# First layer: the S5 columns of the input projection multiplied last, the S5 tables behind all column products, the S5 recurrence and its gated output beside the attention

## Chip, cores and metric

The kernel runs on one core of a Trainium2 chip. The time is device microseconds (us) of one execution, the median of several runs. The engines are named as in the profile: PE (TensorE matmul), PEld (its weight load), DVE (VectorE), ACT (ScalarE), POOL (GpSimd) and SP (SyncE, which issues nearly all transfers). Each engine takes its instructions in a fixed order.

## What is computed

Two layers of a decoder trunk over 1024 tokens of width 1024. One input projection feeds four mixers; the third, S5, is a complex diagonal recurrence with a gated output:

```python
h = rms_norm(x, mix_norm[l])
c_q, c_kv, k_pe, lru_x, lru_gate, s5_u, nsa_q, nsa_kv, nsa_gate = jnp.split(h @ w_in[l], IN_SPLITS, axis=-1)
y_a = mla(c_q, c_kv, k_pe, ...)          # multi-head latent attention
y_b = rglru(lru_x, lru_gate, ...)        # gated linear recurrence
y_c = s5(s5_u, ...)                      # 16 groups of 64 complex states
y_d = nsa(nsa_q, nsa_kv, nsa_gate, ...)  # three-branch sparse attention
y = rms_norm(jnp.stack([y_a, y_b, y_c, y_d], axis=2), out_norm[l])
x = x + y.reshape(x.shape) @ w_out[l]
x = x + hier_moe(rms_norm(x, ffn_norm[l]), ...)

def s5(u, ...):
    # tables from the parameters: powers of the discretised a, bb = g * b
    bu = einsum(u, bb); h = scan(h = ab * h + bu)       # complex
    y = gelu(einsum(h, c) + d * u)
    return y * sigmoid(y @ w_glu + b_glu)
```

## The kernel before

`layer(l, src)` (line 1952) writes one layer as Python generators whose `yield`s interleave the work. Where the text says that something is written earlier or later, this is the order of the program's text; the order that each engine runs is fixed when the program is built, and an instruction written later can stand earlier on its engine when it is ready. A tile comes from a group of buffers of fixed number: 16 of kind `p2` (128x512 fp32, line 128), 4 of kind `p4` (128x1024), 8 each of `wh` and `wl`, and in the stages up to the end of the second token products four PSUM banks `ps1` (line 154). A tile takes a buffer before its first write and gives it back after its last read.

The stages of a layer, in the order of the text before the change:

- In the first layer only, `s5_gen(0, True)` (line 665) first issues the loads of the S5 parameters. Its second part, the S5 tables, follows behind the norm: a chain on DVE (powers of the transition, the rotation tables `phases` for two halves, one on DVE and one on POOL, then for each of four blocks the powers `AC` and `G`), PE transposes and small products, and stores to DRAM (`WA`, `TT`, `KP`). Its tiles are nearly all `p2`. For the second layer the same tables are made beside the experts of the first.
- `mixer_norm` (line 436): eight tiles of x are loaded, normalised, transposed and split into a high and a low part (`hT`). Every fp32 product is made of three matmuls of such parts (lines 181 to 183).
- Column products, `mixer_in` (line 463): 7 groups of 128 columns, each in 2 halves of 512 tokens: 14 units of 24 matmuls into one `ps1` bank each. The groups are 864 and 992 (S5), 352 and 480 (input of the linear recurrence, LRU), 608 and 736 (its gate), 1376 (compressed keys and values). S5 columns are copied to `s5u` (`p4`) and go to DRAM `ud`; LRU columns are copied to `lrux` and `lrug`, which are `p2`, and `lru_piece` (line 615) works on them with about ten more `p2` tiles per piece, in four pieces.
- `s5_run` (line 934): four blocks of `s5_block` (line 879), in three steps each: load the tables and multiply U by `WB` into the one `pto` bank, copy and swap halves by DMA; rotate (two POOL multiplies, one DVE add), four scans on DVE, swap, rotate back; two products per group into `pto`, a gelu, and after two blocks a store to DRAM `vd`. One step is taken per `tick` of the column units from the fourth unit on, and the last ones in the token products.
- First token products, `tok_units(l, 0)` and `mixer_in_tok` (lines 479, 499): 8 tiles of 24 matmuls of 364 columns, each copied to a `p2` tile `z`; `prep_mla` works on `z`. `constants2` and `rope_tables` (lines 238, 316) are written before all columns in the first layer, behind the S5 tables.
- Second token products: 8 tiles of 24 matmuls of 512 columns. `s5_out` (line 943), the gated output of S5, is written from the fourth tile of the first token products on, in two halves of 512 tokens: 24 matmuls of 512 columns, tanh, 16 transposes, stores to DRAM `yd`.
- Attention: `mla_stream` and `nsa_stream`, interleaved by `weave` (line 2064), one step of each per turn. Both gather their values in the one bank `pto`; `mla_values` and `nsa_values` (lines 1363, 1243) hold it with the flag `o_busy`. When the MLA stream ends, `mix_stream` (line 1415) takes its turns: `mix_a(i)` reads 128 rows of `yd` (line 1467), norm, output projection, residual, router.
- `router` and `moe`.

Of the kernel before, what the change touches and what calls it, by code (L numbers as in the profile page):

```python
# [102 lines left out]
class Trunk:  # L103
# [359 lines left out]
    def mixer_in(self, l):  # L463

        w = self.I["w_in"][l].rearrange("(k p) n -> p k n", p=128)
        cols = (864, 992, 352, 608, 480, 736, 1376)
        first = [self.wunit(w[:, :, c:c + 128], 8, 128) for c in cols[:4]]
        yield
        hTh, hTl = self.hT
        for col in cols:  # L470
            wh, wl = first.pop(0) if first else self.wunit(w[:, :, col:col + 128], 8, 128)
            for half in range(2):
                acc = self.ps1()
                for k in range(8):
                    self.mm3(acc, wh[:, k, :], wl[:, k, :], hTh[half][k // 4][:, k % 4], hTl[half][k // 4][:, k % 4],
                             k == 0, k == 7)
                yield col, half, acc
# [401 lines left out]
    def s5_block(self, l, b, io):  # L879
# [12 lines left out]
        WB, AC, TR, TI = WA[:, 0], WA[:, 1], TT[:, 0], TT[:, 1]  # L892
        pt = self.pt("o")
# [27 lines left out]
        yield  # L921
        py = self.pt("o")
# [11 lines left out]
    def s5_run(self, l):  # L934

        io = {}
        blocks = [self.s5_block(l, b, io) for b in range(4)]
        for b in (0, 0, 1, 1, 0, 2, 2, 1, 3, 3, 2, None, 3):
            if b is not None:
                next(blocks[b])  # L940
            yield

    def s5_out(self, l, V):
        nc, v = self.nc, self.nc.vector
        r, w = self.raw(), self.raw(dt=F32R)
        nc.sync.dma_start(r[:, 0:512].rearrange("p (k n) -> p k n", k=2),
                          self.I["s5_w_glu"][l].rearrange("(k p) n -> p k n", p=128))
        self.hi(w[:, 0:512], r[:, 0:512])
        self.lo(w[:, 512:1024], r[:, 0:512], w[:, 0:512])
        wh, wl = [w[:, o:o + 512].rearrange("p (k n) -> p k n", k=2) for o in (0, 512)]  # L950
        for hf in range(2):
            Y, Yh, Yl = self.raw(), self.raw(dt=F32R), self.raw(dt=F32R)
            for k in range(2):
                nc.sync.dma_start(Y[:, 512 * k:512 * k + 512].rearrange("p (t n) -> p t n", t=4),
                                  self.vd[128 * k:128 * k + 128, 4 * hf:4 * hf + 4, :])
            self.hi(Yh, Y)
            self.lo(Yl, Y, Yh)
            Y, Yh, Yl = [[t[:, 512 * k:512 * k + 512] for k in range(2)] for t in (Y, Yh, Yl)]
            yield
            for m in range(2):  # L960
                while self.o_busy:
                    yield
                pt = self.pt("o")
                ms = slice(128 * m, 128 * m + 128)
                for k in range(2):
                    self.mm3(pt, wh[:, k, ms], wl[:, k, ms], Yh[k], Yl[k], k == 0, k == 1)
                t = self.p2(name="glut")
                nc.scalar.activation(t, pt, AF.Tanh, bias=V["hglu"][:, m:m + 1], scale=0.5)
                v.scalar_tensor_tensor(Y[m], t, 1.0, Y[m], op0=ALU.add, op1=ALU.mult)
                yield  # L970
            while self.o_busy:
                yield
            for m in range(2):
                pt = self.pt("o")
                for j in range(4):
                    self.T(pt[:, 128 * j:128 * j + 128], Y[m][:, 128 * j:128 * j + 128])
                o = self.p2((128, 4, 128), name="gluo")
                nc.scalar.activation(o, pt.rearrange("p (j c) -> p j c", j=4), AF.Copy, scale=0.5)
                nc.sync.dma_start(self.yd.rearrange("(n t) c -> n t c", t=8)[:, 4 * hf:4 * hf + 4,
                                                                             512 + 128 * m:640 + 128 * m], o)  # L980
            yield

# [478 lines left out]
    def mix_a(self, i):  # L1461

        nc, mp = self.nc, self.mp
        while self.ndone <= i:
            yield
# [486 lines left out]
    def layer(self, l, src):  # L1952
        nc, tc = self.nc, self.tc
        self.hp = Region(self.bg, f"hT{l}", [("r", [(f"hT{a}{k}{j}", 2048, 1)]) for k in range(2) for a in "hl" for j in range(2)])
        xs, s5 = {}, self.s5_run(l)
# [12 lines left out]
        if l == 0:  # L1968
            gen = self.s5_gen(0, True)
            next(gen)  # L1970
# [4 lines left out]
        if l == 0:  # L1975
            next(units)
            for _ in gen:
                pass
            self.constants2()
            self.rope_tables()  # L1980
        V = self.layer_vectors(l)
        for col, half, pt in units:
# [20 lines left out]
            tick(s5 if col != 864 and (col, half) != (992, 0) else iter(()))  # L2003
        us = self.tok_units(l, 0, V)
        self.nsa_compress(l, V)
        for e in self.mixer_in_tok(us):
            if e:
                later(self.prep_mla(l, *e, V), 1, 2, 3, 4)
                if e[0] == 3:
                    us = self.tok_units(l, 1, V)  # L2010
                    s5 = self.chain(s5, self.s5_out(l, V))
                tick(s5)
# [28 lines left out]
        for _ in s5:  # L2041
            pass
# [11 lines left out]
        self.weave(self.chain(mla, self.mix_stream(l, src)), nsa)  # L2054
# [5 lines left out]
    def chain(self, *gens):  # L2060
        for g in gens:
            yield from g

# [69 lines left out]
```

## Time and profile before

| | us |
|---|---|
| median of 3 runs (lowest, highest) | 2161.67 (2157.28, 2170.07) |
| the profiled execution | 2166.39 |
| its span, first to last instruction | 2164.6 |
| PE busy | 1847.8 (85%) |
| DVE busy | 1309.7 (61%) |
| ACT busy | 1131.7 (52%) |
| POOL busy | 667.5 (31%) |

The profile is of one execution, the slowest core (there is one). Busy times overlap; a matmul's end is modelled, so a busy PE is not a PE at its peak. The first layer runs from 0 to some 1100 us, the second from there on; the two run the same stages but for the S5 tables.

### The profile page before, as it was taken

Reading aid. Unit: us, or ns where it says so; the run is one execution under the profiler, and the core shown is the slowest. Engines: PE = TensorE matmul, PEld = TensorE weight load, DVE = VectorE, ACT = ScalarE, POOL = GpSimd, SP = SyncE. Lnnn points to the kernel's source line nnn. Section 1 sums busy time; section 2 is a strip of 40 time slices with the busy share of each in tenths; the row PEclk is TensorE's granted clock in tenths of the full one; section 3 lists DMA queues with packets and bytes.
Section 4 is the critical chain, followed back from the end, with each engine's and each line's share of the span. In section 5 each row is a group of like instructions: output and inputs, shape, how many; then the busy total and the mean of one; then the engine's idle time right before and its main releaser. Section 6 shows DMA issues by size and latency. Waiting matters only on the chain. (4 is left out here: it accounts for less than half of the span.)

```text
span 2164.6 us, 31426 instructions
## 1 busy us (share of the span) xinstructions
PE 1847.8 (85%) x10386; PEld 1508.6 (70%) x10386; DVE 1309.7 (61%) x2895; ACT 1131.7 (52%) x2474; POOL 667.5 (31%) x1130
## 2 busy tenths in 40 slices
PE   4758899999899977888957789989998999679997
PEld 3647876767677766777856678766676677578886
DVE  5976556577755464776734465565776553746664
ACT  4146544566644435565634555455666543347664
POOL 2432463111111126558711224631111111332221
PEclk9979998699899978999987899986999999789999
DMA  7345442113222337898864354311123123489985
GB/s 218 116 104 134 124 123 62 37 53 73 90 76 80 130 130 193 239 252 244 264 155 148 93 128 124 115 59 37 55 72 94 71 81 139 135 231 289 271 258 124
DMA packets 265966, 293.28 MB, mean 135 GB/s; under 512 B 95416, under 2 KB 222264, under 8 KB 265784
## 3 DMA queue, kind: packets, MB, share of 16 engines
q1 hardware_dynamic: 248568, 243.60, 36.5%
q0 software_dynamic: 16640, 46.43, 10.1%
q8 instruction: 87, 1.43, 0.3%
q10 hardware_dynamic: 576, 1.05, 0.1%
q14 instruction: 95, 0.78, 0.1%
HBM read 215.88 MB, written 79.35 MB: 136 GB/s over the span
## 5 line engine op out<-in xcount | busy, mean ns | idle before, releaser
L177 DVE TENSOR_TENSOR wl<-raw,wh 128x512 fp32r<-128x512 f32 (+3 forms) x294 | 214.6, 758 | 112.0 <-ACT wh L169 110.5
L169 ACT ACTIVATE wh<-raw 128x512 fp32r<-128x512 f32 (+3 forms) x294 | 181.7, 657 | 104.6 <-PE ps L182 55.7
L181 PE MATMUL ps<-mo,wh 128*128 128x256 f32 x576 | 171.3, 297 | 25.2 <-ACT mo L169 25.2
L182 PE MATMUL ps<-mo,wh 128*128 128x256 f32 x576 | 167.8, 292 | 0.2 <-DVE mo L177 0.2
L183 PE MATMUL ps<-mo,wl 128*128 128x256 f32 x576 | 166.3, 290 | 0.0
L1199 DVE TENSOR_REDUCE mx<-ps 128x1 f32<-128x640 f32 (+11 forms) x160 | 132.7, 830 | 50.9 <-PE ps L1233 28.3
L181 PEld LDWEIGHTS ps<-mo,wh 128*128 128x128 f32 x576 | 115.4, 200 | 29.2 <-ACT mo L169 29.0
L169 ACT ACTIVATE mo<-ptt 128x512 fp32r<-128x512 f32 x132 | 76.4, 595 | 105.5 <-PE ptt L214 105.5
L177 DVE TENSOR_TENSOR mo<-ptt,mo 128x512 fp32r<-128x512 f32 x132 | 90.4, 686 | 62.1 <-ACT mo L169 61.7
L177 DVE TENSOR_TENSOR ntl<-ptt,at 128x512 fp32r<-128x512 f32 x132 | 89.1, 686 | 55.5 <-ACT at L169 54.8
L1201 ACT ACTIVATE P<-ps,mx 128x640 f32<-128x640 f32 (+7 forms) x128 | 89.2, 698 | 61.6 <-DVE mx L1199 53.9
L169 ACT ACTIVATE at<-ptt 128x512 fp32r<-128x512 f32 x132 | 76.5, 596 | 82.5 <-PE ptt L214 78.2
L182 PEld LDWEIGHTS ps<-mo,wh 128*128 128x128 f32 x576 | 114.8, 199 | 1.3 <-DVE mo L177 0.5
L183 PEld LDWEIGHTS ps<-mo,wl 128*128 128x128 f32 x576 | 114.7, 199 | 0.0
L202 POOL TENSOR_TENSOR rr<-rv,mhalf 128x1 f32<-128x1 f32 (+5 forms) x98 | 102.1, 1042 | 7.8
L181 PE MATMUL ptx<-wh,mo 128*128 128x512 f32 x240 | 100.8, 420 | 3.4 <-ACT ch L1145 1.7
L214 PE MATMUL ptt<-ident,xg 128*128 128x128 f32 x400 | 64.3, 297 | 41.5 <-DMA xg<-hbuf,mo 38.7
L1815 POOL DMA_INDIRECT xg<-hbuf,mo x50 | 58.0, 1159 | 131.5 <-PE ptt L214 67.1
L181 PE MATMUL ps<-wh,hT 128*128 128x364 f32 (+1 forms) x256 | 97.8, 383 | 0.0
L181 PE MATMUL ps<-hT,wh 128*128 128x512 f32 x224 | 93.8, 420 | 3.5 <-ACT wh L169 3.3
L183 PE MATMUL ptx<-wh,mo 128*128 128x512 f32 x240 | 96.2, 401 | 0.0
L182 PE MATMUL ps<-wl,hT 128*128 128x364 f32 (+1 forms) x256 | 96.0, 375 | 0.0
(636 smaller groups left out, 5805.3 us busy)
## 6 DMA issues: line engine op xcount, KB each, us to landing
raw<-in_moe_w_gate_dram SPq DMA_DIRECT2D x96, 256.0 KB
raw<-in_moe_w_up_dram SPq DMA_DIRECT2D x96, 256.0 KB
mo<-in_moe_w_down_dram SPq DMA_DIRECT2D x32, 512.0 KB
raw<-in_moe_w_down_dram SPq DMA_DIRECT2D x32, 512.0 KB
zm<-mqk SPq DMA_DIRECT2D x16, 512.0 KB
at<-zm SPq DMA_DIRECT2D x16, 512.0 KB
wo<-in_w_out_dram SPq DMA_DIRECT2D x16, 512.0 KB
mo<-yd SPq DMA_DIRECT2D x16, 512.0 KB
```

What stands on the lines that cost most here:

```text
L169: self.nc.scalar.activation(out, in_, AF.Copy)
L177: e.tensor_tensor(out, in_, hi.bitcast(F32), op=ALU.subtract)
L181: mm(out, lh, rh, start=start, stop=False)
L182: mm(out, lh, rl, start=False, stop=False)
L183: mm(out, ll, rh, start=False, stop=stop)
L202: g.tensor_tensor(r, v, self.mhalf[:P, 0:1].to_broadcast([P, k]), op=ALU.pow)
L214: self.nc.tensor.transpose(out, in_, self.ident[:k, :k])
L1199: v.tensor_reduce(mx, S3, axis=AX.X, op=ALU.min)
L1201: nc.scalar.activation(P[j][:, 0:n], S3[:, j], AF.Exp, bias=mx[:, j:j + 1], scale=-1.0, accum_out=acc[:, j:j + 1])
L1815: self.nc.gpsimd.indirect_dma_start(out=xg, out_offset=None, in_=self.hbuf[l], in_offset=bass.IndirectOffsetOnAxis(ap=ix, axis=0), bounds_ ...
```

## The change

In the first layer the column groups are multiplied in the order 352, 608, 480, 736, 1376, 864, 992. The loads of the S5 parameters are written behind the norm and the first weight loads. `constants2`, `rope_tables` and the S5 tables are written behind the last column product and before the first token products. No step of S5 is taken before the second token products; there and in the four turns after them it is one per tile, then one per two turns of `weave` (`sparse`). The four blocks run one after the other instead of interleaved.

In both layers `s5_out` works on four quarters of 256 tokens instead of two halves (48 matmuls of 256 columns in place of 24 of 512), with `p2` tiles instead of `raw`; products into `pto` are put off while `o_busy`; the loop that ran S5 out before the attention's second part is gone, and `mix_a` waits until `s5_out` has ended (`s5_done`).

```diff
@@ mixer_in
-        cols = (864, 992, 352, 608, 480, 736, 1376)
+        cols = (864, 992, 352, 608, 480, 736, 1376) if l else (352, 608, 480, 736, 1376, 864, 992)
@@ s5_block (before the product by WB, and again before the last products)
+        while self.o_busy:
+            yield
         pt = self.pt("o")
@@ s5_run
         io = {}
+        if l == 0:
+            for b in range(4):
+                yield from self.s5_block(l, b, io)
+            return
@@ s5_out
-        for hf in range(2):
-            Y, Yh, Yl = self.raw(), self.raw(dt=F32R), self.raw(dt=F32R)
...
+        r, wh, wl = [self.p2((128, 2, 256), dt, name="gl" + n) for n, dt in (("w", F32), ("wh", F32R), ("wl", F32R))]
...
+        for q in range(4):
+            Y = self.p2((128, 2, 256), name="glY")
             for k in range(2):
-                nc.sync.dma_start(Y[:, 512 * k:512 * k + 512].rearrange("p (t n) -> p t n", t=4),
-                                  self.vd[128 * k:128 * k + 128, 4 * hf:4 * hf + 4, :])
+                nc.sync.dma_start(Y[:, k].rearrange("p (t n) -> p t n", t=2),
+                                  self.vd[128 * k:128 * k + 128, 2 * q:2 * q + 2, :])
+            yield
+            Yh, Yl = [self.p2((128, 2, 256), F32R, name="glY" + n) for n in "hl"]
             self.hi(Yh, Y)
             self.lo(Yl, Y, Yh)
             yield
+            while self.o_busy:
+                yield
+            pt = self.pt("o")
             for m in range(2):
                 ms = slice(128 * m, 128 * m + 128)
                 for k in range(2):
-                    self.mm3(pt, wh[:, k, ms], wl[:, k, ms], Yh[k], Yl[k], k == 0, k == 1)
+                    self.mm3(pt[:, 256 * m:256 * m + 256], wh[:, k, ms], wl[:, k, ms], Yh[:, k], Yl[:, k], k == 0, k == 1)
...
+            nc.sync.dma_start(self.yd.rearrange("(n t) c -> n t c", t=8)[:, 2 * q:2 * q + 2, 512:768], o)
             yield
+        self.s5_done = True
@@ mix_a
-        while self.ndone <= i:
+        while self.ndone <= i or not self.s5_done:
             yield
@@ layer
-        if l == 0:
-            gen = self.s5_gen(0, True)
-            next(gen)
         units = self.mixer_in(l)
         if l:
             next(units)
         self.mixer_norm(l, src)
         if l == 0:
             next(units)
-            for _ in gen:
-                pass
-            self.constants2()
-            self.rope_tables()
+            gen = self.s5_gen(0, True)
+            next(gen)
         V = self.layer_vectors(l)
...
-            tick(s5 if col != 864 and (col, half) != (992, 0) else iter(()))
+            tick(s5 if l and col != 864 and (col, half) != (992, 0) else iter(()))
+        if l == 0:
+            self.constants2()
+            self.rope_tables()
+            for _ in gen:
+                pass
         us = self.tok_units(l, 0, V)
...
-                tick(s5)
+                tick(s5 if l else iter(()))
...
-        for _ in s5:
-            pass
         self.psum(True)
...
-        self.weave(self.chain(mla, self.mix_stream(l, src)), nsa)
+        self.weave(self.chain(mla, self.mix_stream(l, src)), nsa, self.sparse(s5, 2))
...
+    def sparse(self, gen, n):
+        for _ in gen:
+            for _ in range(n):
+                yield
```

## Rows read from the trace of the kernel before

**Rows 1.** Windows: start:end, length, busy PE, PEld, DVE, ACT, POOL, PE clock, DMA, GB/s.

```profile
86.00:135.00 49.00, 22.71 (x138) 18.27 (x136) 40.88 (x87) 10.55 (x16) 19.55 (x56) 0.69 0.52 153
135.00:205.00 70.00, 55.05 (x237) 43.71 (x238) 40.36 (x67) 44.55 (x60) 17.45 (x18) 0.88 0.42 102
...
1191.00:1285.00 94.00, 75.02 (x336) 60.89 (x335) 43.94 (x73) 50.51 (x66) 21.57 (x22) 0.87 0.38 95
```

**Rows 2.** Waits of PE, 78 to 205: line, releaser, total us, times, longest.

```profile
PE ptt L214 <- DVE G L823: 15.6, 3, 8.6
PE pto L926 <- DVE s5B L920: 9.3, 1, 9.3
```

**Rows 3.** Groups by line of PE, 30 to 135: count, busy, mean ns.

```profile
L181 PE MATMUL ps<-hT,wh 128*128 128x512 f32 x66 | 26.8, 409 | 0.2
```

**Rows 4.** Timeline of the first layer's column stage: start, length, instruction, idle before.

```profile
50.81 0.60 ACT L864 ACTIVATE s5u<-ps 128x512 f32<-128x512 f32 x1 [0.23 <-PE ps L183]
51.53 0.15 DVE L303 TENSOR_SCALAR sct<-th 128x16 f32<-128x16 f32 x1
77.91 0.39 PE L182 MATMUL ps<-hT,wh 128*128 128x512 f32 x1
78.14 0.39 PE L183 MATMUL ps<-hT,wl 128*128 128x512 f32 x1
96.19 0.60 ACT L836 ACTIVATE WB<-ptt 128x512 f32<-128x512 f32 x1 [26.55 <-DVE T L822]
102.66 0.40 PE L183 MATMUL ps<-hT,wl 128*128 128x512 f32 x1
121.36 0.18 DVE L852 TENSOR_TENSOR KP<-KP,dI 16x32 f32<-16x32 f32 x1
131.47 1.07 ACT L1990 ACTIVATE lrux<-ps 128x512 f32<-128x512 f32 x2
```

**Rows 5.** Timeline of SP at the start: issue time, length, transfer.

```profile
8.76 0.96 SPq L677 DMA_DIRECT2D sA<-in_s_a_re_dram  x2
...
16.82 1.38 SPq L448 DMA_DIRECT2D xt<-in_x_dram  x3
```

**Rows 6.** Timeline of ACT in the second layer: first LRU copy, last LRU copy.

```profile
1191.19 0.60 ACT L1990 ACTIVATE lrux<-ps 128x512 f32<-128x512 f32 x1 [4.84 <-PE ps L183]
...
1273.72 0.60 ACT L1997 ACTIVATE lrug<-ps 128x512 f32<-128x512 f32 x1
```

**Rows 7.** Waits of PE in the second layer's column stage, 1154 to 1285.

```profile
PE ptx L214 <- POOL u L651: 7.4, 3, 4.9
PE pto L926 <- DVE s5B L920: 4.7, 1, 4.7
PE pto L895 <- DMA s5WA<-s5WA: 4.1, 1, 4.1
```

**Rows 8.** Timeline of the first token products: first copy to z (ACT), last product (PE).

```profile
222.30 0.81 ACT L518 ACTIVATE z<-ps 128x364 f32<-128x364 f32 x2
...
266.66 0.33 PE L183 MATMUL ps<-wh,hT 128*128 128x364 f32 x1
```

**Rows 9.** Timeline: S5's products on PE at full clock, a table load on ACT.

```profile
104.55 1.13 PE L895 MATMUL pto<-U,s5WA 128*128 128x128 f32 x8
...
186.79 0.38 PE L925 MATMUL pto<-U,s5B 128*128 128x128 f32 x2
...
142.99 1.28 ACT L1997 ACT_TABLE_LOAD   x1
```

**Rows 10.** Windows of the attention, first layer, to its MLA end; columns as in Rows 1.

```profile
352.00:548.00 196.00, 181.65 (x948) 134.63 (x947) 138.96 (x339) 118.50 (x309) 38.74 (x100) 0.87 0.22 58
```

**Rows 11.** Timeline: first read of yd by the mix; two expert matmuls of 256 columns.

```profile
545.42 0.80 SPq L1467 DMA_DIRECT2D mo<-yd  x2
...
900.10 0.28 PE L182 MATMUL ps<-mo,wh 128*128 128x256 f32 x1
900.22 0.28 PE L183 MATMUL ps<-mo,wl 128*128 128x256 f32 x1
```

More of the change, by code (lines that the diff above doesn't have):

```diff
@@ L944, in s5_out @@
         nc, v = self.nc, self.nc.vector
[L945 to L950, printed above, removed]
-        for hf in range(2):
-            Y, Yh, Yl = self.raw(), self.raw(dt=F32R), self.raw(dt=F32R)
+        r, wh, wl = [self.p2((128, 2, 256), dt, name="gl" + n) for n, dt in (("w", F32), ("wh", F32R), ("wl", F32R))]
@@ L953, in s5_out @@
+        nc.sync.dma_start(r, self.I["s5_w_glu"][l].rearrange("(k p) n -> p k n", p=128))
+        self.hi(wh, r)
+        self.lo(wl, r, wh)
+        for q in range(4):
+            Y = self.p2((128, 2, 256), name="glY")
             for k in range(2):
-                nc.sync.dma_start(Y[:, 512 * k:512 * k + 512].rearrange("p (t n) -> p t n", t=4),
-                                  self.vd[128 * k:128 * k + 128, 4 * hf:4 * hf + 4, :])
+                nc.sync.dma_start(Y[:, k].rearrange("p (t n) -> p t n", t=2),
+                                  self.vd[128 * k:128 * k + 128, 2 * q:2 * q + 2, :])
+            yield
+            Yh, Yl = [self.p2((128, 2, 256), F32R, name="glY" + n) for n in "hl"]
@@ L956, in s5_out @@
             self.hi(Yh, Y)
             self.lo(Yl, Y, Yh)
-            Y, Yh, Yl = [[t[:, 512 * k:512 * k + 512] for k in range(2)] for t in (Y, Yh, Yl)]
             yield
+            while self.o_busy:
+                yield
+            pt = self.pt("o")
             for m in range(2):
-                while self.o_busy:
-                    yield
-                pt = self.pt("o")
                 ms = slice(128 * m, 128 * m + 128)
                 for k in range(2):
-                    self.mm3(pt, wh[:, k, ms], wl[:, k, ms], Yh[k], Yl[k], k == 0, k == 1)
[L967 to L970, printed above, removed]
+                    self.mm3(pt[:, 256 * m:256 * m + 256], wh[:, k, ms], wl[:, k, ms], Yh[:, k], Yl[:, k], k == 0, k == 1)
@@ L971, in s5_out @@
+            t = self.p2((128, 2, 256), name="glut")
+            for m in range(2):
+                nc.scalar.activation(t[:, m], pt[:, 256 * m:256 * m + 256], AF.Tanh, bias=V["hglu"][:, m:m + 1], scale=0.5)
+            v.scalar_tensor_tensor(Y, t, 1.0, Y, op0=ALU.add, op1=ALU.mult)
+            yield
             while self.o_busy:
                 yield
[L973 to L980, printed above, removed]
+            pt = self.pt("o")
@@ L981, in s5_out @@
+            for j in range(2):
+                for m in range(2):
+                    self.T(pt[:, 256 * j + 128 * m:256 * j + 128 * m + 128], Y[:, m, 128 * j:128 * j + 128])
+            o = self.p2((128, 2, 256), name="gluo")
+            nc.scalar.activation(o, pt.rearrange("p (j c) -> p j c", j=2), AF.Copy, scale=0.5)
+            nc.sync.dma_start(self.yd.rearrange("(n t) c -> n t c", t=8)[:, 2 * q:2 * q + 2, 512:768], o)
             yield
+        self.s5_done = True
     def nsa_compress_in(self, half, pt):
@@ L1954, in layer @@
         self.hp = Region(self.bg, f"hT{l}", [("r", [(f"hT{a}{k}{j}", 2048, 1)]) for k in range(2) for a in "hl" for j in range(2)])
-        xs, s5 = {}, self.s5_run(l)
+        xs, s5, self.s5_done = {}, self.s5_run(l), False
         due, now = [], [0]
@@ L2062, in chain @@
             yield from g
+    def sparse(self, gen, n):
+        for _ in gen:
+            for _ in range(n):
+                yield
     def weave(self, *gens):
```

## The prediction

> **What bounds the kernel now.** I read the windows by stage first. In the first layer the stretch from 86 to 135 us is a hole: PE is busy 22.7 of 49 us at a mean granted clock of 0.69, while DVE is busy 40.9 [rows 1]. Everywhere else in the layer PE is the busiest engine; in the attention it is busy 181.7 of 196 us [rows 10]. So PE bounds the kernel but for this hole, and 135 to 205 still runs at 0.88.
>
> Next come the waits of PE there: 15.6 us for the S5 tables' G and 9.3 us for the S5 recurrence [rows 2]. They are not the whole hole. Column products run without a break at one matmul per 0.23 us (from 77.91 to 78.14 [rows 4]); up to 135 us 64 to 66 of each kind were issued [rows 3], that is 8 units of 24, the last of them at 102.66 [rows 4]. Units 1 to 4 are S5 columns, units 5 to 8 are LRU input and gate, and 8 minus 4 is the number of `ps1` banks. ACT, which has to empty them, sat idle for 26.55 us up to 96.19 and made its first `lrux` copy at 131.47, just after the last table instruction on DVE at 121.36 [rows 4]. A finished product, an idle engine and a copy that doesn't come: what was missing is the copy's `p2` tile. I read this as the tables holding the sixteen `p2` buffers until their end, so that four full banks stop PE. The reading is an inference; no row names a buffer.
>
> The second layer, which makes no tables here, needs 1191.19 to 1273.72 for the eight LRU units [rows 6], with 7.4 us waiting for the LRU's POOL product and 4.7 and 4.1 for S5 [rows 7].
>
> **The change part by part.** The sum runs on one quantity, T, the time at which the tables end; in the profile it is 121.4.
>
> Loads at the start. Between the first S5 load at 8.76 and the first load of x at 16.82 lie 8.06 us of SP's queue [rows 5]. They go behind x and the first weights, so norm and columns start up to 8 us earlier; they can cost something where they now stand between later loads of x, so 0 to 8, and I take 8, since all eight tiles wait for the first.
>
> LRU columns first. The first unit ended at 50.8 [rows 4]; now 43, and it is an LRU unit. The LRU's tiles are written ahead of the tables', so the copies should get their buffers. From first to last LRU copy the second layer took 82.5 us [rows 6]. Of that S5 had 8.8 us of waits [rows 7] and about 12 us of products: a block's first product is 1.13 us and its last pair series runs from 186.79 for 1.7 us, so 2.9 per block [rows 9], four blocks, 11.6. That leaves about 62; last LRU copy at some 103 us.
>
> Tables. They took 51.53 to 121.36, 70 us, a chain of DVE instructions [rows 4]. Now they start when the LRU pieces give buffers back, at about 103, and I take the same 68 to 70: T = 172. Covered by: six more units that need no `p2` (1376, 864, 992; 6 x 24 x 0.23 = 33 us), the first four tiles of the first token products (until the four banks are full; 96 matmuls of 0.17 us, 16 us) and the tables' own PE work. PE thus runs dry a little before 172, not for 50 us. If the chain starts in gaps of DVE before the LRU ends, T is 160; if it starts only when the last LRU piece is done, T is 190.
>
> First token products. Before, the first `z` was copied at 222.3 and the last product issued at 266.7 [rows 8]: 44.7 us. Behind T the same: 172 + 45 = 217, against 267: **50 us earlier** (62 at T = 160, 32 at T = 190). In general the gain is 222 minus T.
>
> `constants2` and `rope_tables` lie in the same stretch as the tables, some 9 us of DVE that were before the columns too; at nothing, covered by the columns; if not, T grows by 9, inside the bounds.
>
> S5 recurrence moved. Its transfers leave the column stage, where SP issued them between weight loads, and stand beside the attention, whose queue is thin (DMA share 0.22 [rows 10]); at nothing, but a swap that waits for a scan holds back the loads queued behind it on SP, those of the attention's tiles. Its POOL multiplies meet an idle POOL (38.7 of 196 [rows 10]). Its PE work, 11.6 us at full clock, now lies where PE is the bound and runs at 0.87: 13.3. Its waits on PE, as in the second layer's column stage, 8.8. Four gelus among the softmax's exponentials switch ACT's table and back, 8 loads of 1.28 us [rows 9] = 10.3 us on an engine busy 118.5 of 196 [rows 10]; I take 4 of them as reaching PE. Together **26 us**. From below: PE is idle 14.4 us in that window, and if S5 fills only that, it costs 0. From above: waits as in the first layer (two times 9) and all of the loads, 42.
>
> The Trainium skill, in "ScalarE: Activation LUTs", section "What ACT_TABLE_LOAD costs", puts a switch at 1.28 us for the load and 1.38 us of drain. The row above shows the load, and the gelu behind it starts 0.02 us after the load's end, so the drain doesn't show here; by the page the loads would be 21 us instead of 10.3, and the cost 30 instead of 26.
>
> Gated output in quarters. The same columns: 48 x 0.12 (expert matmuls of 256 columns [rows 11]) against 24 x 0.23, +0.3 us in each layer. Its work was in the token stages, where PE is as full as in the attention: moved at nothing. In the second layer it ends in the first turns of the weave; +1 for both.
>
> The new wait. In the text, `mix_a` waits for `s5_done`. Counting `yield`s by hand through the generators, S5's last step falls on turn 89 of the weave and the MLA stream ends on turn 94, where the mix first reads `yd` (at 545.42 before [rows 11]). Nothing stands behind that wait then: 0. Each product into `pto` that finds the bank taken puts S5 off by two turns, so the margin is two or three misses.
>
> Sum: -50 + 26 + 1 = **-23 us**. On the profiled execution 2166.4 - 23 = 2143; it lies 4.7 above the median, so on the median 2161.7 - 23 = **2139**.
>
> **The rivals.**
>
> (a) The one bank `pto`. S5 takes it 16 times. Held from the first matmul to the end of the copy, with 0.6 us for a copy, that is 1.7 + 2.3 us per block and about 2.5 + 1.2 us per quarter: 31 us in which neither MLA nor NSA can gather values. For it: in the count, S5's requests find the bank taken nearly every time, so the bank is a bottleneck in its own right. Against: scores and transposes need other banks and can run on. If two thirds of it come on top, -50 + 26 + 1 + 20 = -3: 2159, **no change**.
>
> (b) Slower: the tables stay a wall, only further down. If their first transposes, or their `p2` tiles, come only behind the last column product on PE (103 + 33 = 136), the chain lies bare: T = 136 + 70 = 206, the four banks fill with token products and PE stands again. Then -(222 - 206) + 26 + 1 = +11: 2173. It decides at T = 195, where the sum is zero. For it: this is what the tables did before, and the text writes them behind all columns. Against: instructions stand where they are ready, not where they are written.
>
> (c) S5 costs nothing in the attention (fills the 14.4 us of idle PE): -50 + 1 = -49 at most, with half of the waits -42: 2120.
>
> **How the numbers follow.** The forecast, with T from 160 to 182 and the moved work from 18 to 34, has 0.50 and gives 2124 to 2152. (a) 0.23. (b) 0.15. (c) 0.12. A measurement here can tell some 0.5% (10.8 us) from no change, so faster means below 2150.9. Forecast and (c) lie there but for the forecast's upper edge: 0.60. Within 0.5%: (a) and that edge, 0.25. Slower: (b), 0.15. The range leaves out the far half of (b) and of (c): 2117 to 2173.
>
> **What would show it.** Right: the last table instruction on DVE near 172 and the last product of 364 columns near 217; the first `lrux` copy near 43 with no hole before it; PE's waits for G small; the four scans of block 0 beside the second token products; the first read of `yd` as far behind the last score of MLA as before; from the end of the second token products to the last product of the router some 26 us more than before. Wrong: a stretch in which PE stands with ACT idle behind the columns ((b)); waits of PE on `pto` and turns of MLA longer by a like amount ((a)); a first read of `yd` that comes well after MLA's last values (`s5_done` too late).

## The result, and the profile after

The changed kernel takes 2217.36 us (median of 4 runs, 2211.56 to 2220.34) against 2159.48 for the kernel before on the same chip: a ratio of 1.0239, 95% interval 1.0204 to 1.0274. It is **slower by 2.4%**; the forecast was 2139, faster, with a range up to 2173. The profiled execution is 2218.11 (span 2215.8, mean granted clock 0.889) against 2166.39 (2164.6, 0.902).

The timeline of the changed kernel's first layer answers to [rows 4, 8, 11]; lines behind the edits stand 2 to 9 further down than before. Columns: start, length, engine, line, instruction, idle time before it.

```profile
102.39 0.60 ACT L2001 ACTIVATE lrug<-ps 128x512 f32<-128x512 f32 x1
110.35 0.68 ACT L631 ACTIVATE tt<-ptt,hbi 128x512 f32<-128x512 f32 x1
130.98 0.39 PE L183 MATMUL ps<-hT,wl 128*128 128x512 f32 x1
131.30 0.29 PE L214 MATMUL ptt<-ident,sA 16*128 16x16 f32 x2
131.62 0.17 DVE L698 COPY aR<-ptt 128x16 f32<-128x16 f32 x1 [1.11 <-PE ptt L214]
131.93 0.41 PE L181 MATMUL ps<-wh,hT 128*128 128x364 f32 x1
...
200.83 0.28 DVE L852 TENSOR_TENSOR KP<-KP,dI 16x32 f32<-16x32 f32 x2
208.18 0.81 ACT L518 ACTIVATE z<-ps 128x364 f32<-128x364 f32 x2
252.00 0.33 PE L183 MATMUL ps<-wh,hT 128*128 128x364 f32 x1
...
610.49 0.37 SPq L988 DMA_DIRECT2D yd<-gluo  x1
612.62 0.80 SPq L1476 DMA_DIRECT2D mo<-yd  x2
```

The columns now run through without a hole: the last LRU copy comes at 102.39 (forecast 103) and the last column product at 130.98. But the tables' first transposes on PE stand directly behind that product, and the first table copy on DVE (`aR`) behind them at 131.62. The tables end at 201, and the first `z` is copied at 208. T is 201, not 172.

The windows of the changed kernel by stage (start:end, length, busy time of PE, PEld, DVE, ACT, POOL, PE's granted clock, DMA share, GB/s) answer to [rows 1, 10]:

```profile
33.00:132.00 99.00, 92.54 (x417) 73.53 (x415) 63.13 (x144) 62.38 (x90) 13.56 (x55) 1.00 0.39 92
132.00:208.00 76.00, 35.28 (x213) 31.89 (x211) 58.73 (x195) 9.47 (x21) 25.44 (x56) 0.63 0.26 80
208.00:254.00 46.00, 42.28 (x232) 40.07 (x232) 22.69 (x65) 23.27 (x74) 22.92 (x32) 0.79 0.23 71
254.00:349.00 95.00, 76.47 (x408) 63.29 (x408) 48.94 (x139) 36.33 (x97) 47.58 (x73) 0.91 0.43 127
349.00:592.00 243.00, 209.12 (x1073) 157.24 (x1072) 156.19 (x371) 137.35 (x344) 51.11 (x111) 0.82 0.27 72
592.00:833.00 241.00, 220.06 (x1104) 166.47 (x1104) 132.58 (x247) 115.21 (x263) 32.01 (x61) 0.90 0.31 107
```

Two stages carry the miss. Behind the columns (132 to 208) PE is busy 35.3 of 76 us with ACT at 9.5: the old hole, moved. And the attention up to MLA's last value takes 243 us, against 196 before, with PE at 0.82 instead of 0.87. What PE waits for from 132 to 208 is one thing (total us, times, longest):

```profile
PE ptt L214 <- DVE G L823: 40.4, 4, 30.6
```

The table below has the marks of the first layer in all kernels: T (last table instruction on DVE), first `z` copy, last `z` copy (the second token products' end), MLA's last value, the router's last product. The kernels e4 and e7 start 4 us later than the changed one, because they write zeros first; the text takes that off.

```
kernel                              T   first z  last z  MLA end  router  ratio to before
before                            121    222     351     548      788    1
changed                           201    208     349     592      833    1.0239
e1 tables woven                   192    199     338     581      822    1.0167 (1.0110-1.0225)
e2 S5 late only                   126    201     334     577      822    1.0151 (1.0091-1.0211)
e3 columns only                   202    209     401     596      836    1.0245 (1.0189-1.0300)
e4 no S5                          205    212     332     526      766    (leaves work out)
e5 bank ptx                       201    205     361     600      841    1.0335 (1.0295-1.0374)
e6 POOL's queue                   201    206     350     590      838    1.0263 (1.0217-1.0308)
e7 no gated output                205    210     348     575      808    (leaves work out)
e9 second product unchained       201    208     344     578      826    (leaves work out)
e10 pages and tiles only          202    209     345     564      808    (leaves work out)
e14 pages only                    201    208     342     548      789    (leaves work out)
e13 small tiles                   201    208     355     602      847    1.0304 (1.0242-1.0365)
e15 tables first, small tiles     126    201     344     593      835    1.0224 (1.0165-1.0283)
e8 compression columns third      122    244     372     567      809    1.0078 (1.0049-1.0106)
e11 ten units                     120    233     357     555      796    1.0035 (1.0003-1.0066)
e12 second layer only             123    222     351     547      786    0.9994 (0.9967-1.0020)
```

### The profile page after: what moved, and what is told of

It is laid out like the page before. It is cut to its first block, busy times and chain, and to the rows that moved or that the text cites. A ratio compares the mean times of both kernels' runs of the same rounds, so it can differ in the third digit from the quotient of the medians.

```text
span 2215.8 us, 31564 instructions
## 1 busy us (share of the span) xinstructions
PE 1857.9 (84%) x10434; PEld 1520.6 (69%) x10434; DVE 1313.3 (59%) x2899; ACT 1142.1 (52%) x2492; POOL 660.5 (30%) x1130
## 5 line engine op out<-in xcount | busy, mean ns | idle before, releaser
L177 DVE TENSOR_TENSOR wl<-raw,wh 128x512 fp32r<-128x512 f32 (+4 forms) x294 | 215.4, 760 | 126.7 <-ACT wh L169 124.8
L169 ACT ACTIVATE wh<-raw 128x512 fp32r<-128x512 f32 (+4 forms) x294 | 182.2, 658 | 111.0 <-PE ps L182 56.4
L169 ACT ACTIVATE mo<-ptt 128x512 fp32r<-128x512 f32 x132 | 76.4, 596 | 103.1 <-PE ptt L214 103.0
L182 PE MATMUL ptx<-wl,mo 128*128 128x512 f32 x240 | 96.3, 401 | 0.0
```

The costliest lines, as they stand in the source:

```text
L169: self.nc.scalar.activation(out, in_, AF.Copy)
L177: e.tensor_tensor(out, in_, hi.bitcast(F32), op=ALU.subtract)
L182: mm(out, lh, rl, start=False, stop=False)
```

## The experiments

**The two halves of the change.** e2 puts the column order and the tables back and leaves S5 beside the attention; e3 does the opposite. e4 takes S5 out.

```
e2  cols = (864, 992, 352, 608, 480, 736, 1376)    # both layers
    s5_gen's loads ahead of the norm, the rest of s5_gen, constants2 and rope_tables ahead of the columns
e3  (tables behind the columns)  first token products: if e[0] <= 3: three s5 steps; then s5_out in halves
e4  if l == 0: s5, self.s5_done = iter(()), True   # zeros into yd[:, 512:768]
```

> The changed kernel with the column order and the tables put back as they were before (tables ahead of all columns); only the S5 recurrence and the gated output stand beside the attention. By the prediction's prices (26 for the moved S5, 1 for the quarters, and 9.3 of waits plus 11.6 of products saved in the column stage): about 2162 + 27 - 21 = 2168. Theory W (S5 beside the attention costs 44 up to the end of MLA, the gate of the mix some more, 45 at the end of the router, 9 more in the second layer): about 2162 + 45 + 9 - 21 = 2195, with the end of MLA's values 44 later behind the second token products than before, and the mix waiting for the last store of the gated output.

> The changed kernel with the recurrence and the gated output back in the token stages (all four blocks in the first four turns of the first token products, the output in halves behind it, as before); only the column order and the place of the tables are new. By the prediction's sum without the moved work (50 earlier, less 20 for S5's products and waits that now lie in the token stages): about 2162 - 30 = 2132. Theory W (the tables are a wall that ends at 204 whatever the order, so the stage gains 13, and S5 takes 20 of it back): about 2162 + 7 = 2169, second token products ending at 355 to 366, attention as long as before (196 from the second token products' end to MLA's last value).

> The changed kernel without the first layer's S5 recurrence and gated output (their columns and tables are still made; zeros stand in their place, so what follows the first layer's router works on other values and only the first layer up to the router's end is compared). By the prediction's price of 26 plus 1: router's end at 826 - 27 = 799. Theory W (44 beside the attention, 12 beside the second token products, and what the mix waits): second token products ending at about 338, end of the router at 765 to 775, that is 50 to 60 earlier.

e2 comes out at 1.0151, some 2194 on a kernel before of 2162: theory W. At the router's end of the first layer its trace is 34 us behind the kernel before, and the changed kernel another 11 behind e2. So both halves lose: S5's move 34, and on top of it the columns' and tables' move 11. From the second token products' end to MLA's last value e2 takes 243 us, 46 more than before, as theory W says. e2 also shows the bank reading of the prediction at work: with the tables in front, PE waits 9.8 us for an LRU copy (window 86 to 135):

```profile
PE ptt L214 <- DVE G L823: 21.4, 4, 10.4
PE ps L181 <- ACT lrux L1999: 9.8, 1, 9.8
```

What that copy itself waits for is seen in e2 too: POOL's first write into `gw`, a `p2` tile written just ahead of the LRU's, waits for a product of the tables on PE, as it would for a buffer that the tables still hold, and the first write into `lrux` follows it at 124.88, within 1 us of T. This supports the prediction's reading. The copy comes another 9 us later: on ACT the rope tables' sine and cosine and the gates' weights stand in front of it:

```profile
124.42 0.53 POOL L424 MEMSET gw<- 128x512 f32 x1 [2.83 <-PE ptt L844]
131.94 0.38 ACT L313 ACTIVATE cos<-scr 128x216 f32<-128x216 f32 x1 [1.35 <-DVE scr L312]
133.01 0.63 ACT L169 ACTIVATE gwh<-gw 128x512 fp32r<-128x512 f32 x1 [0.68 <-DMA gw<-in_lru_w_i_dram]
133.54 1.07 ACT L1999 ACTIVATE lrux<-ps 128x512 f32<-128x512 f32 x2
```

e3 missed both expectations: 1.0245 and 401 for the second token products. S5's blocks, written directly behind the tables, stop PE for transfers and the chain (180 to 401):

```profile
PE pto L929 <- DMA s5B<-s5KP: 14.2, 1, 14.2
PE ptt L214 <- DVE G L823: 8.4, 3, 4.4
PE pto L930 <- DVE s5B L922: 8.0, 2, 5.7
```

It says that there is no cheap place for S5 right behind a late T. The attention, with S5 out of it, takes 195 us (401 to 596), as expected. e4's windows, to be set beside the changed kernel's 254 to 349 and 349 to 592:

```profile
258.00:332.00 74.00, 68.29 (x374) 55.55 (x372) 43.05 (x128) 34.21 (x100) 38.19 (x64) 1.00 0.29 95
332.00:526.00 194.00, 178.13 (x948) 131.59 (x948) 138.99 (x339) 118.37 (x310) 38.70 (x100) 0.89 0.21 58
```

Without S5, MLA's last value stands at 522 on the changed kernel's scale instead of 592: S5, blocks and gated output together, costs **70 us** there, more than the 50 to 60 of theory W. The prediction's 26 was for the blocks alone; e7 below splits the 70. From 254 on PE is busy 39 us more (76.5 + 209.1 against 68.3 + 178.1) and idle 31 more (52.4 against 21.6). Busy time multiplied by the granted clock, summed over windows of 1 us, an estimate, gives 244 against 227: some 17 us of work at full clock; the other 22 of the 39 are the same work at a lower clock.

**Where the tables are written.** e1 writes the tables' first steps between the last column units.

```
             tick(s5 if l and ... else iter(()))
+            if l == 0 and col in (1376, 864, 992):
+                next(gen)
```

> The changed kernel, but the first six steps of the S5 tables are written one behind each of the last six column units instead of behind all of them. Theory W (PE takes what is written first, so the tables' first transposes stood behind the last column product although their operands were long there): the first table copy aR, at 131.6 in the changed kernel, comes at 105 to 111, the tables end 20 to 26 earlier (at about 180 instead of 204), and the first token products end that much earlier, at about 230 instead of 254; total about 2217 - 22 = 2195. Rival P (the tables wait for buffers that the LRU pieces give back, the last at 121.4): no table instruction before 121, at most 10 us gained, total 2207 or more. Rival N (the token stages wait for something else): the tables move and the end of the second token products stays near 349.

```profile
112.30 0.17 DVE L698 COPY aR<-ptt 128x16 f32<-128x16 f32 x1 [1.99 <-PE ptt L214]
...
191.37 0.28 DVE L852 TENSOR_TENSOR KP<-KP,dI 16x32 f32<-16x32 f32 x2
...
198.72 0.81 ACT L518 ACTIVATE z<-ps 128x364 f32<-128x364 f32 x2
```

The first table copy moves to 112.30 by the place in the text alone, before 121, so rival P falls. In the changed kernel the loads of the transposes' operands were issued between 40.30 and 50.4, and their bank had been read last at 110.35 (the `tt` copy above); for 20 us PE took column products instead, which are written earlier. In the kernel before, the same copy stands ahead of the norm although it is written behind it; PE was idle then:

```profile
12.34 0.17 DVE L698 COPY aR<-ptt 128x16 f32<-128x16 f32 x1 [8.31 <-PE ptt L214]
```

The size of theory W missed: the chain took 79 us instead of 69 beside the columns and the last of the LRU, so T moved by 9.5. The second token products' end moved by 10.7, and so did the router's end: T is the right variable. The ratio, 1.0167, has an interval that overlaps the changed kernel's a little; the trace is the firmer evidence.

**What S5's 70 us are.** e5 takes the bank, e6 SP's queue, e7 the gated output with the mix's gate.

```
e5  pt = self.pt("o" if l else "x");  while l and self.o_busy: yield      # blocks and gated output
e6  q = nc.sync if l else nc.gpsimd;  q.dma_start(...)                    # all S5 transfers of layer 0
e7  s5_out not chained in layer 0, self.s5_done = True                    # zeros into yd[:, 512:768]
```

> The changed kernel, but in the first layer S5's products and transposes go into the bank ptx instead of pto, and S5 no longer stands aside while MLA or NSA hold pto. From the end of the second token products to MLA's last value the changed kernel takes 243 us, the one before 196, and 194 without S5. Rival (a) (what S5 costs there is the one bank pto): 243 falls to 215 to 225, total about 2217 - 22 = 2195. Theory Q (what it costs is S5's transfers on SP's queue, which hold back the attention's, and PE's own work): 243 stays within 5, total 2212 to 2222; the gated output ends earlier, because it waits for nothing.

> The changed kernel, but all transfers of the first layer's S5 recurrence and gated output are issued on POOL's queue instead of SP's. Theory Q (SP issues in order, so S5's 68 transfers and the swaps that wait for a copy or a scan hold back the loads and stores of the attention's tiles behind them): the first NSA score, 41 us behind the end of the second token products in the changed kernel and 25 without S5, comes 25 to 30 behind; PE's idle time in the attention falls from 34 to about 20; 243 us from the second token products to MLA's last value fall to about 220, total about 2195. Rival (a): unchanged, 2212 to 2222. Rival G (POOL is the worse place, since its own multiplies and the attention's now stand behind the issues): longer than 243, total 2225 or more.

> The changed kernel without the first layer's gated output, and so without the mix's wait for it (zeros stand in its place; only the first layer up to the router's end is compared). The blocks alone remain beside the attention. If the blocks carry the cost (theory Q, since they have nearly all of the transfers and waits): 243 falls to about 225 only, and router's end comes at about 805. If the gated output carries it (rival (a), whose four quarters take pto twice each, or the mix's wait): 243 falls to 210 or less, router's end at 785 or earlier.

e5: with `pto` free of S5 the stretch from the second token products to MLA's last value is 239 us instead of 243, not 215 to 225, and the second token products end 12 us later, at 361 (MLA's end at 600, 1.0335). So rival (a), that the bank `pto` is the cost, falls. e5 moves S5 to another shared bank and does not free it from all banks; `ptx` is the worse one, presumably because the tiles of MLA and NSA are prepared through it, which is not shown. The changed kernel's own trace agrees: from 349 to 592 PE's waits name a copy of S5 out of `pto` once:

```profile
PE pto L1393 <- ACT s5B L904: 1.4, 1, 1.4
```

e5 also bears on the gate. There the gated output's last store is issued at 493.46, 100 us ahead of the mix, and the stretch from MLA's last value to the router's end is 241 us as it is in the changed kernel (833 - 592) and before (788 - 548 = 240). So although the mix's first read at 612.62 stood behind the last store at 610.49, that wait set little. Over all kernels here the stretch is 241 to 248 us, 244 in the mean, where the mix's first read comes behind MLA's end, and 233 to 244, 240 in the mean, where it does not: in the mean the wait is worth some 4 us.

e6: MLA's end moves by 1 us and the first NSA score by 2 (388.5 instead of 390.5): the order of issue on SP is not it, and theory Q falls. POOL is not measurably worse either: the router's end comes 5 us later, and the intervals of the two ratios overlap.

e7: 243 falls to 227, MLA's end to 571 on the common scale: the gated output is 20 us, and of the 16 that lie in the attention 13 are busy time of PE (209.1 against 195.8); the blocks are the other 49. This is what its expectation had for blocks that carry the cost, the router's end included (804 on the common scale, forecast 805). Up to there the gated output is 29 us, since part of it lies behind MLA's end.

> The changed kernel, but in the first layer the second product of each S5 block reads operands that lie ready (the block's own table page and U) instead of the result of swap, multiplies and scan, so PE never waits for that chain. Everything else of the block still runs; the recurrence is thus left out of the result, and only the first layer up to the router's end is compared. Theory H (PE takes its instructions in a fixed order and stands in front of S5's second products while the chain runs, and the clock falls with it): the 243 us from the second token products to MLA's last value fall to 220 to 228, and the second token products end at 340 instead of 349. Rival B (S5's pages and its U and Yo tiles take buffers from the token stage and the attention): 243 stays within 5, 349 too.

> The changed kernel, but the first layer's S5 blocks only take their pages and tiles, load them, hold them over the same three turns with two POOL multiplies in place of the chain, and store; their products, swaps, scans and gelus are left out (so only the first layer up to the router's end is compared). The gated output stays. Rival B (buffers): 243 falls by no more than the blocks' own work, to 228 to 235, and the second token products end near 345. Theory H (PE's standing in front of the chain): 243 falls to about 194 + 16 = 210, second token products at 330.

> The kernel e10_pages_only without U and Yo: the S5 blocks take, load and hold their pages alone, and the store goes from a page (again only the first layer up to the router's end is compared). e10 ended the second token products at 345 and MLA's values at 564; without any S5 block or gated output they stand at 328 and 522 on the same scale. Theory B4: 330 to 334, and 545 to 550. Rival Bp: 345 and 564 within 4.

```
e9   nc.tensor.matmul(o, WB[:, g] if l == 0 else TD[:, g], U[...]);  matmul(o, AC[:, g], U[...] if l == 0 else s[:, g])
e10  load pages, U; yield; B = WB*TR, X = AC*TI on POOL; yield; Yo = B*U, X*U on POOL; store; yield; return
e14  as e10 without U and Yo; the store goes from B
```

Windows of e9, of e10 and of e14, each from the last first-token product on, split at the last `z` copy (e9's first):

```profile
254.00:344.00 90.00, 74.95 (x407) 61.98 (x407) 48.31 (x139) 36.19 (x96) 47.48 (x72) 0.91 0.47 134
344.00:578.00 234.00, 205.78 (x1073) 156.29 (x1073) 155.06 (x370) 136.79 (x345) 51.39 (x111) 0.83 0.28 75
```

```profile
254.00:345.00 91.00, 70.97 (x359) 57.74 (x359) 45.34 (x123) 31.86 (x89) 50.36 (x74) 0.87 0.44 131
345.00:564.00 219.00, 201.39 (x1027) 153.34 (x1028) 150.31 (x358) 128.13 (x338) 49.05 (x109) 0.81 0.26 69
```

```profile
254.00:342.00 88.00, 73.95 (x375) 60.43 (x375) 47.54 (x131) 34.29 (x100) 54.43 (x78) 0.90 0.42 133
342.00:547.00 205.00, 187.25 (x1010) 140.77 (x1010) 146.00 (x350) 125.40 (x326) 39.52 (x100) 0.88 0.26 69
```

By MLA's end, from nothing upwards: 522 (e4), 548 with pages and gated output (e14), 564 with U and Yo (e10), 592 with products and chain (changed). Of the last 27, 13.5 go when the second product no longer waits for the chain (e9), half of what theory H expected. U and Yo have 17, products, swaps and scans 27. The first 26 are pages and gated output together; if the gated output costs the 20 of e7 here too, the pages are left with some 5. Neither H nor B alone: the price is spread. Theory B4 is half right at best: e14 has MLA's end at 548 as it says, but the second token products end at 342, not at 330 to 334. The steps were taken away in one order only, so each share is the one in that order, and how thinly S5's steps are spread over the attention's turns was not varied.

> The changed kernel, but in the first layer each S5 block has its own U and Yo of 512 columns in p2 buffers (of which there are 16) instead of two blocks sharing U and Yo of 1024 columns in p4 buffers (of which there are 4); twice as many transfers of half the size. Theory B4 (U and Yo hold half of the p4 buffers, in which the token stage and the attention keep mqk, sqm and mq): the second token products end at 335 to 338 instead of 349, total about 2217 - 15 = 2202. Rival Bp (S5's pages in wh and wl, or its transfers, do it): 349 stays within 3, total 2215 or more.

> The kernel e2_s5_late_only (tables ahead of all columns as before, S5 late) with the small tiles of e13_small_tiles: the best of the parts, if they add. e2 ran at 1.0151 of the kernel before, with the second token products ending at 334. Theory B4 and additive parts: they end at 320 to 323, ratio about 1.008. Rival Bp: no gain on 1.0151.

e13 gives each block its own tiles from the larger set (`U, Yo = p2(128, 4, 128)`, twice the transfers). It is slower (1.0304), with the second token products' end at 355 where neither theory had it: the loads of U now come when PE already waits for them (254 to 355):

```profile
PE pto L903 <- DMA U<-ud: 11.3, 1, 11.3
PE pto L936 <- DVE s5B L928: 5.3, 1, 5.3
```

e15, the same on e2, gains nothing either (1.0224 against e2's 1.0151, second token products' end at 344 instead of 334). So whether U and Yo cost their 17 us by holding `p4` buffers or by their transfers stays open; no kernel with more `p4` buffers was run.

**The hole itself.** e8 and e11 start from the kernel before.

```
e8   cols = ... if l else (864, 992, 1376, 352, 608, 480, 736);  s5 blocks one after the other
e11  e8's columns; weights of five columns ahead (cols[:5]); s5 steps only behind the last four units, three each,
     blocks in the order (0, 0, 1, 1, 0, 1, 2, 2, 3, 3, 2, 3)
```

> The kernel before the change with one edit of order: in the first layer the compression columns (1376), whose copies need no p2 buffer, are multiplied third instead of last, and the four S5 blocks are written one after the other. Theory B of the hole (four filled banks stop PE because the copies of LRU units wait for p2 buffers until the tables end at 121): ten units instead of eight are multiplied before 121, two units of 24 products of 0.23 us = 11 us earlier from there on, so column products end at about 192 instead of 203 and the total is 2162 - 11 = 2151 (ratio 0.995). Rival: PE takes what is written first, and S5 blocks written one after the other expose their waits in the column stage (9 us as before, or more): ratio 1.00 or above.

> The kernel before the change with three edits of order in the first layer: the compression columns are multiplied third, the weights of five columns instead of four are loaded ahead, and the S5 steps, whose pages are of the same two sets as the weights, are written into the last four column units, three steps each. In e8_compress_early only eight units ran before the tables ended, since the fifth column's weights came at 137 to 145. Theory: with the weights there, ten units run before 121, and column products end 11 us earlier than before at 192, total about 2162 - 11 = 2151. Rival: S5's steps, three at a time, expose their waits in the column stage as in e8: 2170 or more.

e8 missed its theory: column products end at 214, not at 192, and the ratio is 1.0078. Again 192 products (eight units) ran before 131 us, although two more copies needed no `p2` tile. The fifth column's weights were late; the DVE half of their split, in e8:

```profile
145.00 1.20 DVE L177 TENSOR_TENSOR wl<-raw,wh 128x1024 fp32r<-128x1024 f32 x1
```

and in the kernel before:

```profile
140.37 1.20 DVE L177 TENSOR_TENSOR wl<-raw,wh 128x1024 fp32r<-128x1024 f32 x1
```

That is behind the first `lrux` copy of 131.47 [rows 4]. In the kernel before, unit 9's first four products, which need only the high part of the weights, run at 133.25, right behind that copy; the next one, which needs the low part, runs at 141.63:

```profile
133.25 0.48 PE L181 MATMUL ps<-hT,wh 128*128 128x512 f32 x1
141.63 0.80 PE L183 MATMUL ps<-hT,wl 128*128 128x512 f32 x1 [2.99 <-DVE wl L177]
```

So unit 9 had two reasons to wait: up to the copy the bank would have held it by itself, and the weights held the rest of it some 8 us longer. In e2, where S5 takes no pages in this stage, they were split from 52 on and the copies were the wait. e11 has the weights in time and 244 products before 131, ten units as the bank reading says; column products end at 173 instead of 203. Yet the token stage doesn't start earlier (first `z` copy at 233 instead of 222): S5's steps, now written behind, hold PE for the LRU and the chain. Ratio 1.0035 (1.0003 to 1.0066): the hole is filled and nothing is gained, with S5's steps moved in the same edit; filling it alone was not run. No version here beats the kernel before.

**The second layer.** e12 has the first layer of before and the second of the changed kernel.

> The kernel before the change in the first layer, the changed one in the second (gated output in quarters, the waits for pto, the sparse weave, the gate of the mix). The prediction's term for it is 1 us at most: 2163, ratio 1.0005. Rival: the traces show the changed kernel's second layer 9 us longer (1025.6 before, 1034.6 after, from the norm to the end): 2171, ratio 1.004, the first half of it between the norm and the router.

0.9994 (0.9967 to 1.0020): in the second layer quarters, sparse weave and gate cost nothing that can be measured. The 9 us between the two traces in that layer lie outside this interval, so they are not the edit's alone; where they come from stays open.

## Why the prediction was wrong, step by step

- **Columns first, LRU early: right in effect, the number by luck.** Last LRU copy at 102.4 for a forecast 103, no hole before 132. But the first copy came at 57.4 instead of 43, behind a load of the gates' weights, and the eight copies took 45 us instead of 62; the two errors cancel (and 43 + 62 is 105, not 103). The loads of x do start 8 us earlier, as forecast (8.67 instead of 16.82).
- **The reading of the hole was half right.** Filled banks are one limit (e2, e11), the fifth column's weights another, which in the kernel before ends later (e8). The first copy comes not at the tables' end but 8 to 10 us behind it, since ACT has the rope tables' sine and cosine and the gates' weights in front of it (e2). The prediction saw eight units and took the bank count as the only way to get eight; four columns of weights loaded ahead give eight too.
- **Tables start at 103, T = 172: the first step that failed.** T was 201 and rival (b) had 206. Its condition, first transposes behind the last column product, is what the trace shows (131.30), and its argument against, "instructions stand where they are ready", is what e1 refutes for a busy engine: ready at 110, they were taken at 131 because PE had earlier-written work. It holds where the engine is idle: in the kernel before, the same copy stood at 12.34. The chain itself took 69 us as forecast. The prediction also let the first `z` follow T at once; it came 7 us later, while ACT stood for the products of NSA's compressed keys (6.59 us up to 207.18). The gain at the first token products was 267.0 - 252.3 = 15 us instead of 50, and 29 of the missing 35 are T. From e2 one sees that even this was no gain: with S5 late, tables in front are 11 us better than tables behind. The overlap is what counts: in front, the tables cover 44 us of columns (8 units, 192 products of 0.23); behind, they cover 16 us of token products, until four banks are full.
- **Moved S5 at 26 us: the second step that failed, a term mis-sized; the blocks measured 49 (e7 against e4), with the gated output 70.** The sum had the products (13.3), 8.8 of waits and 4 of table loads. For blocks and gated output together the work is some 17 us at full clock, near the 11.6 and 48 x 0.12 = 5.8 of the prediction's rows. What failed are the waits: the profile has 31 us more of idle PE, and some 22 more from a lower clock, which beyond the 0.87 of before had no term. "Transfers at nothing" was right for SP's queue (e6), and wrong for what U, Yo and their loads cost (17). ACT loads a table 7 times from 252 to 592 and once without S5: 6 x 1.28 = 7.7 us, near the 10.3 of the prediction, of which it took 4. The Trainium skill's drain of 1.38 us per load, in "ScalarE: Activation LUTs", section "What ACT_TABLE_LOAD costs", again doesn't show: `lrug` at 102.39 starts 0.02 us after a load that began at 101.09 and took 1.28, and that load began 0.01 us after the activation before it had ended (100.46 + 0.62).
- **Gated output +1: right in the second layer** (e12), wrong in the first. There it is 20 us of the 70. "Moved at nothing" gives 8 of them back: the second token stage, 267.0 to 351.4 = 84 us before with the second half of the gated output in it, takes 76 without any S5 (e4, 255.4 to 331.8). Its first half stood in the first token stage, whose gain is counted above. The move cost some 12 us net.
- **The new wait at 0: nearly right in effect, wrong in the count.** The last store came after MLA's end (610 against 592), but the mix's tail is 241 us in e5 without that wait too, and over all kernels the wait is worth some 4 us in the mean.
- **Rival (a)** is out as far as the bank `pto` goes (e5). **Rival (b)** had the mechanism of T and a chance of 0.15; with S5 at 26 it ended at 2173, well below the result, because it shares the mis-sized term.

The measured terms add up at MLA's end: 548 before, - 15 (first token products), - 8 (second token stage without the gated output, 84.4 to 76.4), - 2 (attention without S5, 196 to 194), + 49 (blocks), + 20 (gated output) = 592, as in the trace: 44 us later, where the prediction had 23 earlier. Of the 67 between, T and the gap to the first `z` have 35, the blocks 23, the gated output's move 11. From there on the layer is as long as before within 2 us, and with the 9 us of the second layer's trace, which e12 doesn't confirm as the edit's, less 3 in the first layer's experts, the profiled execution is 51 us longer.

## What to carry to other kernels

In these kernels a chain that starts with one small instruction on a full engine starts where that instruction is written (131), not where its operands are ready (110); on an engine with nothing older to do it started early (12). So before moving such a chain, look which older work the engine still has, and write the chain's first step ahead of it. The price of work moved beside a full engine is not its own time: here some 17 us of products cost 70, most of it as idle time and as a lower clock, so price it by a kernel that leaves the work out before pricing its parts. And when a count has one explanation (eight units, four banks), look for the second resource that gives the same count.

## What the hardware showed that was not expected

The granted clock stayed low after the pauses that came before it were over. From 132 to 208, where PE was busy 35.3 of 76 us, the mean clock was 0.63, between the levels of 1.2 GHz (0.5) and 2.4 GHz (1.0). In windows of 4 us it stood at 0.50 in each from 152 to 220, though PE had been busy for 19.7 of the 20 us from 200 on. Over the 46 us from 208, with PE busy for 42.3, the mean was still 0.79. In the attention the mean was 0.82 over 243 us with S5's stops, and 0.89 over 194 without S5; that lower clock, some 22 us from 254 on by the estimate above, cost two thirds as much as the stops themselves (31).
